# Rows of the last four experts by products with a 0/1 matrix, scatters that do not wait for each other, and a 512-wide second MLP

## The chip, the cores and the metric

The kernel runs on one core of a Trainium2 chip, as one program in one launch. The metric is device time in microseconds (us). The kernel before took 2708.14 us, the median of three runs (2706.81 to 2711.54). The execution that the profiler recorded took 2708.97 us, of which 2707.1 us are the span between the first and the last instruction.

## The reference

512 tokens of width 1024 pass through a hybrid block (state space branch, window attention, and a mixture of experts) and then through a two-layer block with 16 meta tokens ahead of the 512.

```python
def hier_moe(h2, ...):                       # h2: 512 x 1024
    ...                                      # router: two experts of 64 for each token, with a weight each
    def expert_block(args):
        xb, e = args
        hid = jax.nn.silu(xb @ w_gate_e[e]) * (xb @ w_up_e[e])    # 1024 x 256 each
        return hid @ w_down_e[e]                                  # 256 x 1024
    ys = lax.map(expert_block, (xs, block_e)).reshape(n_rows, -1)
    return jnp.zeros_like(h2).at[tok].add(ys * wt[:, None])       # weighted rows back to their tokens
...
def squared_relu_mlp(x, g, w_in, w_out):
    h = rmsnorm(x, g)
    return jnp.square(jax.nn.relu(h @ w_in)) @ w_out              # 1024 -> 4096 -> 1024
...
# second block: h = [meta; x + moe]; h += stick-breaking attention (a_w_qkv, a_w_o); h += mlp 0;
#               h += differential attention; h += mlp 1; the 512 token rows are the output
```

All values are float32. Nothing but the 512 x 1024 result leaves the chip.

## The kernel before

The first block takes the span up to about 700 us, the router and the experts the stretch to about 1300, attention A the stretch to 1660, MLP 0 to 2020, attention B to 2340, and MLP 1 the rest. A framework orders the instructions of each engine once, when the program is built, by its own estimate of durations; `pin` keeps an instruction in program order. Engines then run their lists in that order and wait for each other on semaphores, so an instruction that stands late in its engine's list makes everything wait that needs it.

**Experts.** Each expert has 48 slots. A group of five experts is gathered together: products of a 0/1 matrix `perm` with the tokens (line 787, 16 matmuls in four of five experts) give `xg`, the tokens of the slots, turned. For expert e, `expert_m` (line 928) makes gate and up by 16 float32 matmuls (32 in the trace, where each takes two passes); ACT makes silu (line 935, `lo`), DVE the product (line 936, `sg`); PE turns it (line 943), an engine copies it to `hT`; `expert_d` (line 955) makes the 48 x 1024 result one expert later. ACT and DVE copy its two halves to one of three buffers `ys` (lines 958 and 959), and POOL scatters these rows to the DRAM tile `y_d` with an indirect DMA (line 898). All scatters write the one tile `y_d`, and the framework makes each wait until the one before has landed.

**Weights.** 192 loads of 1 MB on SP's queue (line 910) go into a ring of 14 tiles, in the order in which PE uses them; a load waits for the matmuls that last read its tile.

**Combination.** When all is scattered, SP loads `y_d` back by 8 loads (line 739), DVE multiplies by the token's two weights and adds to `x2` (line 745, 16 instructions 128x512), PE turns the sums (line 750), and `hT` goes to attention A. Its first projections (line 229) need the first `a_w_qkv` weights split into two parts `wh` and `wl` (lines 179 and 180) and the scaled tokens split into `hh` and `hl` (lines 209 and 210).

**MLP 1.** All products with split operands are three matmuls (high by high, low by high, high by low, line 229). In MLP 1 each of them is 256 wide: the first layer takes the 512 tokens in two spans (`HX`), the second takes 256 columns of `w_out` at a time, over eight slices of the 1024 hidden values of a chunk.

## Time and profile before

| what | us |
|---|---|
| median of three runs | 2708.14 |
| profiled execution | 2708.97 |
| its span | 2707.1 |
| first expert to last expert's products | 760 to 1271 |
| last product to attention A at full clock | 1271 to 1320 |
| MLP 1 | 2340 to 2707 |

PE is busy in 94% of the span, with a mean granted clock of 0.977. A granted clock of 1.00 is 2.4 GHz, 0.50 is 1.2 GHz. The trace names its queues and engines as the page does: PE the matrix engine, PEld its weight loads, DVE, ACT and POOL the others, SP the queue of plain DMAs. In a row "idle before" stands in brackets with the instruction that ended it.

### The profile page before, as it was taken

Reading aid. Unit: us, or ns where it says so; the run is one execution under the profiler, and the core shown is the slowest. Engines: PE = TensorE matmul, PEld = TensorE weight load, DVE = VectorE, ACT = ScalarE, POOL = GpSimd, SP = SyncE. Lnnn points to the kernel's source line nnn. Section 1 sums busy time; section 2 is a strip of 40 time slices with the busy share of each in tenths; the row PEclk is TensorE's granted clock in tenths of the full one; section 3 lists DMA queues with packets and bytes.
Section 4 is the critical chain, followed back from the end, with each engine's and each line's share of the span. In section 5 each row is a group of like instructions: output and inputs, shape, how many; then the busy total and the mean of one; then the engine's idle time right before and its main releaser. Section 6 shows DMA issues by size and latency. Waiting matters only on the chain.

```text
span 2707.1 us, 46829 instructions
## 1 busy us (share of the span) xinstructions
PE 2533.1 (94%) x18850; PEld 2180.6 (81%) x18850; DVE 1546.9 (57%) x3266; ACT 1089.3 (40%) x2249; POOL 537.8 (20%) x534
## 2 busy tenths in 40 slices
PE   7998999999889999986789889999999899999999
PEld 5987769879855555543788789999999777899999
DVE  6488676696542222221699887334557878644433
ACT  5356644442311111111477655223335766523321
POOL 0044532130101011111144330001201445100000
PEclk9999999999989999998799999999999999999999
DMA  5233365545399999994411323222231111322221
GB/s 191 90 112 123 108 218 174 174 140 195 110 411 398 419 409 398 415 412 167 177 56 32 102 69 130 87 94 94 94 115 63 32 56 51 115 85 91 93 93 63
DMA packets 111436, 436.92 MB, mean 161 GB/s; under 512 B 16505, under 2 KB 37545, under 8 KB 68976
## 3 DMA queue, kind: packets, MB, share of 16 engines
q1 hardware_dynamic: 105552, 429.20, 43.3%
q0 software_dynamic: 5520, 4.63, 0.7%
q8 instruction: 150, 2.46, 0.4%
q14 instruction: 70, 0.57, 0.1%
q10 hardware_dynamic: 144, 0.07, 0.0%
HBM read 400.52 MB, written 43.79 MB: 164 GB/s over the span
## 4 chain that ended last, share of the span: by engine, by line
PE 52%; DVE 9%; ACT 3%; DMA 3%; issue 2%; POOL 0%; POOLq 0%; DVEq 0%; ACTq 0%; SPq 0%
PE pd L229 35%; PE pd L928 7%; DMA y_d<-ys,idx 3%; PE pm L787 3%; PE pm L955 3%; DVE zd L1927 1%; PE pd L242 1%; DVE wl L180 1%; DVE zt L1915 1%; DVE zd L1916 1%; PE pm L2425 1%; PE pm L943 1%; PE pm L229 1%; PE pm L242 0%; ACT zt L1917 0%
## 5 line engine op out<-in xcount | busy, mean ns | idle before, releaser
L229 PE MATMUL pd<-hh,wh 128*128 128x256 f32 (+2 forms) x1408 | 436.7, 312 | 12.0 <-ACT hh L209 8.5
L229 PE MATMUL pd<-hh,wl 128*128 128x256 f32 (+2 forms) x1408 | 436.9, 311 | 1.0 <-DVE wl L242 1.0
L229 PE MATMUL pd<-hl,wh 128*128 128x256 f32 (+2 forms) x1408 | 436.1, 311 | 0.9 <-DVE hl L210 0.9
L206 ACT ACTIVATE wh<-raw 128x1024 fp32r<-128x1024 f32 (+2 forms) x228 | 222.7, 1022 | 402.6 <-PE pd L229 301.8
L207 DVE TENSOR_TENSOR wl<-raw,wh 128x1024 fp32r<-128x1024 f32 (+2 forms) x228 | 280.3, 1260 | 155.6 <-ACT wh L206 155.4
L229 PEld LDWEIGHTS pd<-hh,wh 128*128 128x128 f32 x1408 | 266.7, 190 | 26.7 <-ACT hh L209 9.2
L229 PEld LDWEIGHTS pd<-hl,wh 128*128 128x128 f32 x1408 | 267.3, 190 | 15.9 <-DVE hl L210 1.6
L229 PEld LDWEIGHTS pd<-hh,wl 128*128 128x128 f32 x1408 | 266.9, 190 | 15.5 <-DVE wl L242 1.9
L229 PE MATMUL pd<-wh,hh 128*128 128x256 f32 (+2 forms) x936 | 266.7, 285 | 4.4 <-DVE vt L2273 1.8
L229 PE MATMUL pd<-wl,hh 128*128 128x256 f32 (+2 forms) x936 | 264.1, 282 | 2.2 <-DVE wl L210 2.2
L229 PE MATMUL pd<-wh,hl 128*128 128x256 f32 (+2 forms) x936 | 264.2, 282 | 0.0
L928 PE MATMUL pd<-mraw,xg 128*48 128x256 f32 x2048 | 237.9, 386 | 0.0
L928 PEld LDWEIGHTS pd<-mraw,xg 128*48 128x48 f32 x2048 | 128.5, 124 | 90.1 <-issue 12.8
L229 PEld LDWEIGHTS pd<-wh,hh 128*128 128x128 f32 (+1 forms) x936 | 170.3, 182 | 10.2 <-issue 2.7
L229 PEld LDWEIGHTS pd<-wl,hh 128*128 128x128 f32 (+1 forms) x936 | 170.2, 182 | 4.5 <-DVE wl L210 2.7
L229 PEld LDWEIGHTS pd<-wh,hl 128*128 128x128 f32 (+1 forms) x936 | 170.0, 182 | 1.9 <-issue 0.2
L898 POOL DMA_INDIRECT y_d<-ys,idx x64 | 60.8, 950 | 474.1 <-DMA y_d<-ys,idx 222.3
L229 PE MATMUL pd<-vh,wl 128*128 128x272 f32 (+1 forms) x512 | 145.1, 284 | 0.0
L229 PE MATMUL pd<-vl,wh 128*128 128x272 f32 (+1 forms) x512 | 144.9, 284 | 0.0
L229 PE MATMUL pd<-vh,wh 128*128 128x272 f32 (+1 forms) x512 | 143.7, 285 | 0.0
L229 PE MATMUL pd<-wl,vh 128*128 128x256 f32 x512 | 143.1, 281 | 0.0
L229 PE MATMUL pd<-wh,vh 128*128 128x256 f32 x512 | 143.0, 281 | 0.0
(573 smaller groups left out, 6269.4 us busy)
## 6 DMA issues: line engine op xcount, KB each, us to landing
mraw<-in_w_moe SPq DMA_DIRECT2D x192, 1024.0 KB
raw<-in_mlp_w_in SPq DMA_DIRECT2D x32, 1024.0 KB
raw<-in_mlp_w_out SPq DMA_DIRECT2D x32, 1024.0 KB
raw<-in_w_xbc SPq DMA_DIRECT2D x12, 1024.0 KB
raw<-in_a_w_qkv SPq DMA_DIRECT2D x12, 1024.0 KB
raw<-in_w_z SPq DMA_DIRECT2D x8, 1024.0 KB
raw<-in_w_gate_in SPq DMA_DIRECT2D x8, 1024.0 KB
bc<-acT_d SPq DMA_DIRECT2D x32, 256.0 KB
```

Source lines behind the costliest of these rows:

```text
L180: self.nc.vector.tensor_tensor(l[:, x], raw[:, x], h[:, x].bitcast(F32), op=ALU.subtract)
L206: nc.scalar.activation(h, src, AF.Copy)
L207: nc.vector.tensor_tensor(l, src, h.bitcast(F32), op=ALU.subtract)
L229: self.nc.tensor.matmul(*a, **kw)
L242: return lambda *a, **kw: pin(f(*a, **kw))
L787: self.pin(nc.tensor.matmul(p[:, 256 * i:256 * i + 256], lhsT=x[2 * t + k // 4][:, (k % 4 + i) * 128:(k % 4 + i + 1) * 128], rhs=perm[:, t ...
L898: self.nc.gpsimd.indirect_dma_start(out=self.y_d[:, :], out_offset=bass.IndirectOffsetOnAxis(ap=rows, axis=0), in_=y[0:64 + self.CAP], in_ ...
L928: self.pin(self.nc.tensor.matmul(p[64 * i:64 * i + self.CAP, 0:256], lhsT=x[:, k], rhs=w[i][:, k], start=k == 0, stop=k == 7))
L943: self.pin(nc.tensor.transpose(pt[:, f * 128:f * 128 + 128], sg[:, f * 128:(f + 1) * 128], self.ident))
L955: self.pin(nc.tensor.matmul(py[64 * m:64 * m + CAP, :], lhsT=hT[:, f * CAP:(f + 1) * CAP], rhs=wd[:, 1024 * f + 512 * m:1024 * f + 512 * m ...
L1915: nc.vector.tensor_scalar(t[:, :n], z[:, :n], 40.0, None, op0=ALU.min)
L1916: nc.vector.tensor_scalar(d[:, :n], z[:, :n], 40.0, 0.0, op0=ALU.subtract, op1=ALU.max)
```

## The change

Six edits:

- The scatters of experts 0 to 59 are declared independent of each other; each waits only for the fourth before it. Experts 60 to 63 are not scattered: four scatters of zero rows, placed at expert 2, fill their places in `y_d`.
- Experts 60 to 63 work in pairs: two experts' `sg` are turned into one tile `hz`, `expert_pair` makes both results (128 slots x 1024), scales them by `last_w` and splits them into `ysp`; `combine` adds them to the turned `x2` in PSUM by products with a 0/1 matrix `last_p` (tokens by slots). `last_rows` builds both from the router's slots, at expert 60.
- `y_d` (4 loads instead of 8) and `x2` are loaded, multiplied and added during the last experts, and the first weights of attention A are loaded among the last expert weights and split at expert 63. The function table load of ACT moves to expert 63 as well.
- From weight number 171 on the ring has the 7 `mr` tiles only.
- A few small instructions of attention A and B are pinned.
- MLP 1 uses 512-wide matmuls: one span in the first layer, 512 columns of `w_out` and four hidden slices at a time in the second; `w_out` is laid out anew outside the kernel.

```diff
-                if e:
+                if 0 < e <= 60:
                     self.expert_d(h, e - 1)
+                if e == 62:
+                    self.expert_pair(hz, 0)
                 if g < NG - 1:
...
+                if e == 63:
+                    self.pin(nc.scalar.preload_act_table_set("natural_log_exp_and_others"))
...
-                h = self.expert_t(sg)
+                if e < 60:
+                    h = self.expert_t(sg)
+                else:
+                    self.expert_t(sg, hz[e // 2 - 30][:, e % 2])
...
+                    for j in range(60, 64):
+                        self.scatter(self.ys[2], self.idx[:, j:j + 1], 1)
...
+                    hz = [self.cb.tile([128, 2, 2, 64], F32, name=f"hz{j}") for j in range(2)]
+                    for j in range(2):
+                        nc.gpsimd.memset(hz[j], 0.0)
+                    self.ysp = [self.cb.tile([128, 2, 1024], F32R, name=f"ysp{j}") for j in range(2)]
...
+                    x2 = [self.cb.tile([128, 2048], F32, name="x2a"), self.st_tile("wl")]
...
+                if e == 60:
...
-            self.expert_d(h, 63)
+                    self.last_rows()
+                if e == 61:
+                    ys = []
+                    for t in range(4):
+                        ys.append(self.st_tile(("raw", "raw", "wh", "raw")[t]))
+                        if t == 0:
+                            self.ahead(self.a_units())
+                        y = nc.sync.dma_start(ys[t].rearrange("p (k c) -> p k c", k=2),
+                                              self.y_d.rearrange("(k t p h) c -> t p k (h c)", k=2, t=4, h=2)[t])
+                        self.after(y, self.scattered)
+                    for t in range(4):
+                        for i in range(2):
...
+                                V.scalar_tensor_tensor(x2[t][:, c], ys[t][:, 1024 * k + 512 * i:1024 * k + 512 * i + 512], self.gw[k][:, t:t + 1], x2[t][:, c],
...
+                if e == 63:
+                    for _ in range(4):
+                        self.tick()
+            self.expert_pair(hz, 1)
...
+    def last_rows(self):
+        nc = self.nc
+        V = self.PV
+        Q, Q1 = [self.mp.tile([128, 4, 256], F32, tag="perm", bufs=2, name="lastq") for _ in range(2)]
+        for t in range(4):
+            for k, x in enumerate((Q, Q1)):
+                V.tensor_scalar(x[:, t], self.lastc, self.slot_of[:, 4 * k + t:4 * k + t + 1], self.gw[k][:, t:t + 1], op0=ALU.is_equal, op1=ALU.mult)
+            V.tensor_tensor(Q[:, t], Q[:, t], Q1[:, t], op=ALU.add)
+        self.last_w = self.mt.tile([128, 2], F32, name="lastw")
+        self.last_p = self.mp.tile([128, 2, 512], F32R, tag="perm", bufs=2, name="lastp")
+        for j in range(2):
+            p = self.P()
+            for t in range(4):
+                self.pin(nc.tensor.transpose(p[:, 128 * t:128 * t + 128], Q[:, t, 128 * j:128 * j + 128], self.ident))
+            V.tensor_reduce(self.last_w[:, j:j + 1], p, axis=AX.X, op=ALU.add)
+            V.tensor_scalar(self.last_p[:, j], p, 0.0, None, op0=ALU.is_gt)
...
+    def expert_pair(self, hz, j):
+        nc = self.nc
+        e = 60 + 2 * j
+        wd = [self.moe_raw(e + x, 2) for x in range(2)]
+        for m in range(2):
+            p = self.P()
+            for f in range(2):
+                for x in range(2):
+                    self.pin(nc.tensor.matmul(p[64 * x:64 * x + 64, :], lhsT=hz[j][:, x, f], rhs=wd[x][:, 1024 * f + 512 * m:1024 * f + 512 * m + 512],
+                                              start=f == 0, stop=f == 1))
+            c = slice(512 * m, 512 * m + 512)
+            self.split_to(self.ysp[j][:, 0, c], self.ysp[j][:, 1, c], p, self.last_w[:, j:j + 1])
...
+        ps = {}
+        def turn(k):
+            ps[k] = self.P()
+            for t in range(4):
+                self.pin(nc.tensor.matmul(ps[k][:, 128 * t:128 * t + 128], lhsT=x2[t][:, k * 128:(k + 1) * 128], rhs=self.ident, start=t == 0, stop=False, skip_group_check=True))
+        turn(0)
+        turn(1)
+        for k in range(8):
+            p = ps.pop(k)
+            for j in range(2):
+                for x in range(2):
+                    self.pin(nc.tensor.matmul(p, lhsT=self.ysp[j][:, x, k * 128:(k + 1) * 128], rhs=self.last_p[:, j], start=False, stop=j == 1 and x == 1, skip_group_check=True))
+            nc.vector.tensor_copy(hT[k][:, 16:528], p)
+            if k < 6:
+                turn(k + 2)
...
+    def scatter(self, y, rows, free=0):
...
+        if free:
+            for o in self.scattered:
+                self.tc.declare_no_dep(x.ins, o.ins, reason="the rows of two blocks are disjoint")
+            if len(self.scattered) > 3:
+                self.after(x, [self.scattered.pop(0)])
+            self.scattered.append(x)
...
+    def next_ring(self):
+        return self.ring[self.mn % len(self.ring)] if self.mn < 171 else ("mr", self.NMP)
...
-    HX = ((16, 272), (272, 528))
+    HX = ((16, 528),)
...
-                W = self.load_split(I["mlp_w_out"][layer, 4 * c + u], 2048)
+                W = self.load_split(I["mlp_w_out"][layer, 4 * c + u], 2048, 4 if last else 8)
...
+                    n, x = divmod(u, 2)
+                    if not x:
+                        out = [self.PD() for _ in range(4)]
                     for t in range(4):
-                        d = acc[t][u // 2][:, (u % 2) * 256:(u % 2) * 256 + 256]
-
...
+                        ts = slice(128 * t, 128 * t + 128)
+                        self.mm3(out[t], lambda k: hid[0][4 * x + k][:, ts], lambda k: hid[1][4 * x + k][:, ts], lambda k: W[0][:, k], lambda k: W[1][:, k],
+                                 K=4, start=not x, stop=x == 1)
+                        if x:
+                            d = acc[t][n]
+                            V.scalar_tensor_tensor(d, out[t], rc[:, t:t + 1], d, op0=ALU.mult, op1=ALU.add)
+                            if c == 3:
+                                nc.sync.dma_start(self.O[128 * t:128 * t + 128, 512 * n:512 * n + 512], d)
```

The lists that the program is built to differ in three places that matter here. First SP's queue from the experts' weights to attention A, before and then after (`w_moe` expert weights, `x_d` the tokens, `y_d` the scattered rows, `a_w_qkv` attention A's weights).

```order
L910 DMA mraw<-in_w_moe 128x2048 x145
L718 DMA meta<-in_meta 16x1024
L910 DMA mraw<-in_w_moe 128x2048 x17
L717 DMA mraw<-x_d 128x1024 x4
L739 DMA mraw<-y_d 128x1024 x8
L140 DMA raw<-in_a_w_qkv 128x2048 x2
```

```order
L1009 DMA mraw<-in_w_moe 128x2048 x140
L745 DMA mraw<-x_d 128x1024 x2
L727 DMA meta<-in_meta 16x1024
L1009 DMA mraw<-in_w_moe 128x2048 x8
L142 DMA raw<-in_a_w_qkv 128x2048
L1009 DMA mraw<-in_w_moe 128x2048 x5
L741 DMA a_norm_g<-in_a_norm_g 128x8
L745 DMA x2a<-x_d 128x1024 x2
L1009 DMA mraw<-in_w_moe 128x2048 x9
L759 DMA mraw<-y_d 128x2x1024 x4
L142 DMA raw<-in_a_w_qkv 128x2048 x2
```

The loads of `x_d`, of the first `a_w_qkv` and of `a_norm_g` moved in among the last 22 expert weights; the loads of `y_d` stand behind the last of them as before.

Then PE's list ahead of attention A: before from expert 61's products on, after from the end of expert 60 on (`sg` products to be turned, `lastq` the tile behind `last_p`, `mraw` weights, and in the row of line 750 the sums).

```order
L928 MATMUL pd<-mraw,xg 48x256 x16
L955 MATMUL pm<-mraw,hT 48x512 x4
L943 MATMUL pm<-consts,sg 128x128 x2
L928 MATMUL pd<-mraw,xg 48x256 x16
L955 MATMUL pm<-mraw,hT 48x512 x4
L943 MATMUL pm<-consts,sg 128x128 x2
L722 MATMUL pm<-consts,meta 128x16 x8
L928 MATMUL pd<-mraw,xg 48x256 x16
L955 MATMUL pm<-mraw,hT 48x512 x4
L943 MATMUL pm<-consts,sg 128x128 x2
L955 MATMUL pm<-mraw,hT 48x512 x4
L750 MATMUL pm<-consts,mraw 128x128 x32
```

```order
L1057 MATMUL pm<-mraw,hT 48x512 x4
L1042 MATMUL pm<-consts,sg 128x128 x2
L749 MATMUL pm<-consts,meta 128x16 x8
L799 MATMUL pm<-consts,lastq 128x128 x8
L1027 MATMUL pd<-mraw,xg 48x256 x16
L1042 MATMUL pm<-consts,sg 128x128 x2
L1027 MATMUL pd<-mraw,xg 48x256 x16
L813 MATMUL pm<-mraw,hz_11792 64x512 x8
L1042 MATMUL pm<-consts,sg 128x128 x2
L1027 MATMUL pd<-mraw,xg 48x256 x16
L1042 MATMUL pm<-consts,sg 128x128 x2
L813 MATMUL pm<-mraw,hz_11793 64x512 x8
```

The 16 matmuls of an expert (`pd<-mraw,xg`) stand in both; the products with `hT` behind each of them have gone from expert 61 on, two groups of eight with `hz` have come, and ahead of expert 61 stand eight transposes of `lastq`. Behind the last row of after come 32 products with the identity (line 826) and 32 with `last_p` (line 833), in turns, and then attention A.

Last DVE's list from the product of expert 60 (before) and from the end of `last_rows` (after) to the first additions (`wl` the low part of attention A's first weights, `ysp` the low part of a pair's result).

```order
L936 TENSOR_TENSOR sg<-lo,pd 48x256
L959 COPY ys<-pm 48x512
L936 TENSOR_TENSOR sg<-lo,pd 48x256
L256 COPY hT<-pm 128x96
L936 TENSOR_TENSOR sg<-lo,pd 48x256
L959 COPY ys<-pm 48x512 x3
L745 SCALAR_TENSOR_TENSOR mraw<-mraw,gw_8083 128x512 x2
L745 SCALAR_TENSOR_TENSOR mraw<-mraw,gw_8084 128x512 x2
```

```order
L126 TENSOR_SCALAR lastp<-pm 128x512
L1061 COPY ys<-pm 48x512 x2
L1035 TENSOR_TENSOR sg<-lo,pd 48x256 x2
L213 SCALAR_TENSOR_TENSOR ysp_11796<-pm,lastw,ysp_11796 128x512
L259 COPY hz_11793<-pm 128x2x48
L213 SCALAR_TENSOR_TENSOR ysp_11796<-pm,lastw,ysp_11796 128x512
L1035 TENSOR_TENSOR sg<-lo,pd 48x256
L183 TENSOR_TENSOR wl<-raw,wh 128x512 x4
L213 SCALAR_TENSOR_TENSOR ysp_11797<-pm,lastw,ysp_11797 128x512
L766 SCALAR_TENSOR_TENSOR x2a<-mraw,gw_8083,x2a 128x512 x2
L766 SCALAR_TENSOR_TENSOR x2a<-mraw,gw_8084,x2a 128x512
L213 SCALAR_TENSOR_TENSOR ysp_11797<-pm,lastw,ysp_11797 128x512
```

Before, the additions to the sums came after the last copies of `ys`. Now the split of a pair's result, the `wl` part and three of the 16 additions stand ahead of the last pair's second split, and 13 additions behind it.

## Rows read from the trace of the kernel before

**Rows 1.** the page, engines' busy time, and the chain that ended last, by line

```profile
PE 2533.1 (94%) x18850; PEld 2180.6 (81%) x18850; DVE 1546.9 (57%) x3266; ACT 1089.3 (40%) x2249; POOL 537.8 (20%) x534
PE pd L229 35%; PE pd L928 7%; DMA y_d<-ys,idx 3%; PE pm L787 3%; PE pm L955 3%; DVE zd L1927 1%; PE pd L242 1%; DVE wl L180 1%; DVE zt L1915 1%; DVE zd L1916 1%; PE pm L2425 1%; PE pm L943 1%; PE pm L229 1%; PE pm L242 0%; ACT zt L1917 0%
```

**Rows 2.** by stretch: us, engines busy, granted clock, DMA share, GB/s

```profile
1160.00:1200.00 40.00, 36.00 (x272) 21.16 (x270) 10.57 (x21) 6.10 (x15) 4.72 (x5) 1.00 1.00 406
1200.00:1245.00 45.00, 29.33 (x183) 15.77 (x180) 6.63 (x13) 6.46 (x13) 5.66 (x6) 0.85 0.77 309
1300.00:1320.00 20.00, 12.13 (x47) 10.76 (x48) 15.04 (x31) 13.98 (x26) 4.55 (x3) 0.50 0.70 255
...
2400.00:2500.00 100.00, 100.00 (x847) 100.00 (x846) 39.65 (x61) 27.80 (x42) 0.00 (x0) 1.00 0.28 96
```

**Rows 3.** PE's timeline: start, duration, work, idle before; experts 10, 20, 56, 57, 60

```profile
837.99 1.29 PE L928 MATMUL pd<-mraw,xg 128*48 128x256 f32 x10
...
910.41 0.86 PE L928 MATMUL pd<-mraw,xg 128*48 128x256 f32 x6
...
1196.20 3.66 PE L928 MATMUL pd<-mraw,xg 128*48 128x256 f32 x32
1203.83 3.66 PE L928 MATMUL pd<-mraw,xg 128*48 128x256 f32 x32
1219.56 0.69 PE L943 MATMUL pm<-consts,sg 128*128 128x128 f32 x2 [8.25 <-DVE sg L936]
1245.25 3.66 PE L928 MATMUL pd<-mraw,xg 128*48 128x256 f32 x32
```

**Rows 4.** what PE waited for, 880 to 1160 us: total, times, longest

```profile
PE pm L787 <- DVE ys L959: 6.1, 7, 0.9
PE pm L943 <- DVE xg L256: 5.3, 7, 0.8
PE pm L943 <- ACT xg L254: 4.6, 7, 0.7
```

**Rows 5.** what ACT waited for, 1160 to 1245 us

```profile
ACT ys L958 <- DMA y_d<-ys,idx: 35.9, 6, 7.8
```

**Rows 6.** the chain of waits, 1160 to 1325 us: start, duration, what

```profile
1163.41 7.74 DMA y_d<-ys,idx
1171.91 6.69 DMA y_d<-ys,idx
...
1277.14 2.59 DMA y_d<-ys,idx
1279.79 3.79 DMA mraw<-y_d
...
1293.45 1.99 DVE mraw L745 x3
```

**Rows 7.** line 910, weight loads issued before 1200 us

```profile
L910 SPq DMA_DIRECT2D mraw<-in_w_moe x180: 327/328/1588, 707.1 to 1199.9; - x180
```

**Rows 8.** groups of instructions by line and shape, 1060 to 1160 us

```profile
L955 PE MATMUL pm<-mraw,hT 128*48 128x512 f32 x112 | 26.4, 592 | 0.0
L936 DVE TENSOR_TENSOR sg<-lo,pd 48x256 f32<-48x256 f32 x14 | 5.9, 422 | 44.6 <-ACT lo L935 44.6
L124 DVE TENSOR_SCALAR perm<-iota,slots 128x256 fp32r<-128x256 f32 x11 | 3.9, 353 | 0.4
```

**Rows 9.** the same, 1245 to 1320 us

```profile
L745 DVE SCALAR_TENSOR_TENSOR mraw<-mraw,gw 128x512 f32<-128x512 f32 x16 | 10.9, 745 | 11.4 <-DMA mraw<-y_d 11.4
L750 PE MATMUL pm<-consts,mraw 128*128 128x128 f32 x32 | 7.3, 403 | 20.1 <-issue 14.9 <-DVE mraw L745 5.1
L210 DVE SCALAR_TENSOR_TENSOR hl<-hT,a_norm_g,hh 128x528 fp32r<-128x528 f32 x8 | 6.7, 873 | 0.1
```

**Rows 10.** PE's timeline of 512-wide matmuls at full clock, 20 from first to last

```profile
36.83 0.39 PE L229 MATMUL pd<-hh,wl 128*128 128x512 f32 x1
...
41.26 0.39 PE L229 MATMUL pd<-hh,wh 128*128 128x512 f32 x1
```

More of the change, by code (lines that the diff above doesn't have):

```diff
@@ L724, in moe @@
                         nc.scalar.activation(hT[k][:, 0:16], pm[:, k * 16:(k + 1) * 16], AF.Copy)
-            self.expert_d(h, 63)
+                    self.last_rows()
[10 more added lines that the diff above has]
+                        for i in range(2):
+                            c = slice(512 * i, 512 * i + 512)
+                            for k in range(2):
+                                V.scalar_tensor_tensor(x2[t][:, c], ys[t][:, 1024 * k + 512 * i:1024 * k + 512 * i + 512], self.gw[k][:, t:t + 1], x2[t][:, c],
+                                                       op0=ALU.mult, op1=ALU.add)
@@ L726, in moe, with st_tile, a_units @@
+                if e == 63:
+                    for _ in range(4):
+                        self.tick()
+            self.expert_pair(hz, 1)
             self.combine(hT, x2)
+            cb.close()
         return hT
+    def st_tile(self, tag):
+        return self.st.tile([128, 2112], F32, tag=tag, bufs=dict(self.ring)[tag], name="mraw")[:, :2048]
+    def a_units(self):
+        W = self.I["a_w_o"]
+        return [(self.I["a_w_qkv"][i + hg], 2048, 8) for hg in range(4) for i in (0, 4, 8)] + [(W[u][:, :1280], 1280, 5) for u in range(4)] \
+            + [(W[u][:, 1280:], 768, 3) for u in range(4)]
@@ L894, in overflow, with after @@
                     self.scatter(y, rc)
-    def scatter(self, y, rows):
-        self.nc.gpsimd.indirect_dma_start(out=self.y_d[:, :], out_offset=bass.IndirectOffsetOnAxis(ap=rows, axis=0), in_=y[0:64 + self.CAP], in_offset=None,
-                                          bounds_check=2047, oob_is_err=False)
+    def after(self, ins, others):
+        for x in others:
+            self.tc.add_manual_dep(ins.ins, x.ins.name, mybir.DependencyInfo(mybir.DependencyClass.Sync, mybir.DependencyReason.DATA), reason="rows")
+    def scatter(self, y, rows, free=0):
+        x = self.nc.gpsimd.indirect_dma_start(out=self.y_d[:, :], out_offset=bass.IndirectOffsetOnAxis(ap=rows, axis=0), in_=y[0:64 + self.CAP], in_offset=None,
+                                              bounds_check=2047, oob_is_err=False)
+        if free:
[4 more added lines that the diff above has]
+            self.scattered.append(x)
     NMP = 7
     ring = [("raw", 3)] * 3 + [("wh", 2), ("wl", 2)] * 2 + [("mr", NMP)] * NMP
+    def next_ring(self):
+        return self.ring[self.mn % len(self.ring)] if self.mn < 171 else ("mr", self.NMP)
     def moe_load(self, n):
@@ L913, in moe_tile @@
     def moe_tile(self):
-        tag, b = self.ring[self.mn % len(self.ring)]
+        tag, b = self.next_ring()
         self.mn += 1
@@ L1675, in layer_a @@
         self.klz = self.kl_tiles([self.la.tile([128, T2], F32R, tag="kl", bufs=2, name="klz") for _ in range(2)])
-        W = self.I["a_w_o"]
-        self.ahead([(self.I["a_w_qkv"][i + hg], 2048, 8) for hg in range(4) for i in (0, 4, 8)] + [(W[u][:, :1280], 1280, 5) for u in range(4)]
-                   + [(W[u][:, 1280:], 768, 3) for u in range(4)])
         self.rest([self.qkv(0, xs, r, sets[0], late)])
```

77 lines of the change are left out of this document (33 added, 44 removed).

## The prediction

> **What bounds the kernel now.** I read the page first: PE is busy 94% of the span, but the chain that ended last holds 3% of it, some 80 us, in scatters [rows 1], so a part of the experts is bound by something else. The table by stretch says where (its columns are PE, PEld, DVE, ACT and POOL): from 1160 to 1200 us PE is busy 36.0 of 40 us at full clock, from 1200 to 1245 only 29.3 of 45 at a clock of 0.85, and from 1300 to 1320 it has 47 instructions at a clock of 0.50, while MLP 1 is PE from end to end [rows 2]. PE's timeline dates the experts. Ten experts from 10 to 20 take 72.42 us, 7.24 each, which is the pace without waits (7.63 with a gather, as 56 to 57, and less in each fifth). From 20 to 57 the 37 experts take 293.42, which is 25.5 above 37 x 7.24. The three from 57 to 60 take 41.42, with one gap of 8.25 us alone [rows 3].
>
> These two losses differ. Between 880 and 1160 us PE's waits are short, 0.8 to 0.9 us, for copies by DVE of an older expert's results [rows 4]: such copies stand behind the newer expert's product in DVE's list. Between 1160 and 1245 ACT waits 35.9 us for scatters to land before it may write `ys` again [rows 5]. The chain there is one scatter after the other, 1163.41 to 1171.15, 1171.91 to 1178.60 and on like that, and at the end again until 1279.79, when the loads of `y_d` start [rows 6].
>
> **Independent scatters.** Without gaps the three experts from 57 to 60 take 7.63 + 7.63 + 7.63 less one gather (2.0; expert 59 has none) = 20.9 us. So 41.42 - 20.9 = 20.5 us go, if ACT finds its buffer free. A scatter lands in 6.7 to 7.7 us with the weights streaming [rows 6]; with three buffers and a pace of 7.24 it has two experts' time, 14.5 us, and the wait for the fourth before it asks less still. The short waits do not go. By the lists, between experts 20 and 59, gathers, transposes and products with `hT` still wait for an older expert's copy: I count 46 gathers and transposes of that kind before and 43 after. I leave the 25.5 us as they are. What is late next is DMA, which works at a share of 1.00 and 406 GB/s up to 1200 us [rows 2]: 180 of the weights were issued by 1199.9 [rows 7], one in 2.6 us, and expert 60 needs numbers 180 and 181 and the three other megabytes queued ahead of them, so it could start at 1199.9 + 5 x 2.6 + 2.6 = 1215.5 at the earliest. Expert 60 starts at 1245.25 - 20.5 = 1224.8 in my sum. I call this T. The ends are 1215.5 and 1245.
>
> **Experts 60 to 63, from T.** Products 3.66 [rows 3], silu, product and turn to T + 6.3. Then `last_rows`, which the trace does not have: eight comparisons at 0.353 and four additions, taken at the 0.422 of a product of the same width [rows 8], 4.5 us of DVE with PE waiting, as the transposes of `lastq` stand ahead of expert 61; with them T + 12.3. Expert 60 to 61 so takes 12.3 in place of 5.8, and what waits behind it on PE is everything. Two more products: T + 20. A pair's 16 passes at 0.236 [rows 8] take 3.8: T + 24; they take the place of four experts' `hT` products and cost nothing more. The ring of seven tiles lets the last weight go when the first pair is done, T + 24; it lands 2.6 later, and the four loads of `y_d`, queued behind it, at about T + 29.5, 32, 34.5 and 37. Expert 63's products end at T + 28, ACT then has silu, table load and `hz`, and the second pair ends at T + 35. On DVE the last split is ready at T + 36, and 13 of the 16 additions stand behind it at 0.745 [rows 9]: 9.7 us, T + 45.5. Only then does the turning of `x2` have all it needs.
>
> **The combination.** 32 products with the identity: the 32 transposes of before took 7.3 us [rows 9] while the clock fell to the 0.50 of 1300 us [rows 2], so 4 to 7.3; I take 6. 32 products 128x512 with `last_p`, at the step of 512-wide matmuls at full clock, (41.26 - 36.83) / 19 = 0.233 [rows 10]: 7.5. PE was nearly idle from T + 35 to T + 45.5; in the kernel before the clock stands at 0.50 after such a stretch [rows 2], so I add 4 (bounds 0 and 13.5, all at half clock). Copies and splits (0.87 each, [rows 9]) run beside it. Attention A starts at T + 45.5 + 17.5 = T + 63, about T + 64 with its first wait: 1289.
>
> Before, attention A had done by 1320 us 47 instructions in 12.13 us at half clock [rows 2], worth 6.1 at full clock: a start at 1313.9. Weights of attention A are now split beforehand, its stuttering start goes with that. The gain so far is 1313.9 - 1289 = 25. Of this 20.5 is the scatters and 4.5 the tail: what pairs and early loads save (no scatters at the end, 1261 to 1279.8, and no splits of weights behind the combination) is mostly paid back by `last_rows`, by the additions behind the second pair and by 64 products for 32 transposes.
>
> **MLP 1.** 847 matmuls 256 wide in 100 us are 0.1181 each [rows 2]. 3072 of them become 1536 at 0.233: 362.7 - 358.2 = 4.5 us. The PE-bound stretch has no other limit: DVE is busy 40 of 100 us. The Trainium skill, "TensorE: Matmul & The Clock Gate", section "Back-to-back issue gap", gives each isolated matmul a fixed 2.5 ns above its columns; by that this edit would be worth 1536 x 2.5 ns = 3.8 us. The rows give 4.5 and I keep them. The other edits, pins and the earlier `a_norm_g`, I put at 0, between -3 and 3: PE waits in neither attention for one of them in a way I could name.
>
> **Sum.** 2708.97 - 25 - 4.5 = 2679.5 by the profiled execution, 0.83 above the median of three; against runs I say 2679.
>
> **Rivals.**
> 1. The short waits go too. With no chain of scatters the copies come earlier than the lists suggest, and only DMA bounds: T = 1215.5, 9 less: 2670. For it: the lists were made for other durations than the chip's. Against: the waits in [rows 4] come from DVE's order alone, and scatters had no part in them.
> 2. The scatters stay one behind the other. They share POOL's queue; if that takes them one at a time at 7 us, ACT keeps about half of its wait, 10 us: 2689. No row has two scatters in flight; their distance of 7.5 us in [rows 6] is set by the wait that goes. The Trainium skill, "DMA: Bandwidth & Descriptors", section "Two DMAs through the same engine are not ordered", says that descriptors of a queue start in order but are pipelined. No row here shows it; it speaks against this rival.
> 3. Slower: the ring of seven tiles starves PE. From expert 57 on a load waits for a tile freed 2.3 experts earlier. If the loads fell back by more than that, each of seven experts would cost three loads in a row and its products, 7.8 + 3.7 = 11.5, instead of 6.9 on average: 7 x 4.6 = 32 us, 2711. It decides from the point where a load lands over 16 us after its tile came free; at 2.6 us a megabyte and four extra megabytes in between that is 13 us at worst, so it should not.
> 4. The change to the experts is worth nothing: the 20.5 us come back in the tail, where the additions or the first splits stall at half clock (13.5 instead of 4, and `y_d` 3.8 us a load [rows 6] instead of 2.6, and 6 more in the start): 2679 + 9.5 + 5 + 6 = 2700.
>
> **Chances and range.** The forecast 0.55, rival 1 0.17, rival 2 0.13, rival 4 0.08, rival 3 0.07. The range takes in rivals 1 and 2 with the bounds of the combination (4 less, 9.5 more) and most of rival 4: 2660 to 2700. The forecast's own is 2672 to 2690. Under 0.2%, 5.4 us, a measurement of this kernel does not tell a change from none: faster 0.88, same 0.05, slower 0.07.
>
> **What would show it.** ACT's wait for `y_d` gone and expert 60 at 1225; about 12 us from expert 60 to 61; 13 additions in a row ahead of the first product with the identity; attention A from its first product at full clock near 1289; MLP 1 with 512-wide matmuls every 0.233 us and PE still 100% busy. It is wrong if expert 60 starts after 1235, if PE waits for weights from expert 57 on, or if MLP 1 gets gaps in which PE waits for a wider tile.

## The result, and the profile after

The kernel after takes 2679.72 us (median of 4 runs, 2677.19 to 2681.70), the kernel before 2709.27 (4 runs, 2706.81 to 2711.54): a ratio of 0.9891, 95% interval 0.9873 to 0.9908. The forecast of 2679 is met in the sum. The stages will show that of its three terms the first is right in the sum though not in its parts, the second (MLP 1) is too small, and the third, the tail behind the experts, has the wrong sign.

The busy times on the page of the kernel after, beside [rows 1]. The chain that ended last can be followed back only to 1294.6 us here, behind the experts, so it says nothing of the scatters; ACT's waits below do.

```profile
PE 2529.9 (95%) x17386; PEld 2111.9 (79%) x17386; DVE 1546.4 (58%) x3218; ACT 1082.4 (40%) x2209; POOL 536.9 (20%) x536
```

Its table by stretch answers to [rows 2]; the columns are the same (stretch, length, PE, PEld, DVE, ACT, POOL with their counts, granted clock, DMA share, GB/s).

```profile
1160.00:1200.00 40.00, 38.38 (x291) 23.28 (x292) 10.28 (x21) 6.40 (x15) 5.64 (x6) 1.00 0.94 368
1200.00:1223.00 23.00, 21.47 (x161) 12.06 (x159) 5.34 (x11) 5.45 (x11) 4.33 (x6) 1.00 0.95 382
1223.00:1252.00 29.00, 23.04 (x145) 11.53 (x144) 11.13 (x24) 4.77 (x18) 3.77 (x4) 0.88 0.89 355
1252.00:1293.00 41.00, 29.38 (x148) 19.88 (x147) 24.72 (x40) 10.09 (x16) 0.00 (x0) 0.83 0.62 233
1293.00:1313.00 20.00, 16.77 (x109) 15.91 (x107) 11.67 (x17) 9.70 (x19) 6.00 (x7) 0.83 0.19 70
2370.00:2470.00 100.00, 100.00 (x434) 81.23 (x433) 39.48 (x45) 27.46 (x34) 0.00 (x0) 1.00 0.29 102
```

Up to expert 60 PE is now busy at full clock (38.4 of 40 us, then 21.5 of 23). The loss has moved: between 1223 and 1293 PE has 52.4 busy us of 70, at a clock of 0.88 and 0.83. MLP 1 still fills PE, with 434 wide matmuls where there were 847.

What ACT waited for, 1160 to 1230 us. Beside [rows 5], the 35.9 us for scatters are gone; ACT now waits for PE, as an engine does that keeps up.

```profile
ACT lo L1034 <- PE pd L1027: 32.2, 9, 5.5
ACT hT L257 <- PE pm L1042: 13.5, 4, 4.7
ACT xg L257 <- PE pm L871: 12.4, 4, 3.4
```

What PE waited for, 883 to 1163 us, answers to [rows 4]: most of the short waits for copies stayed (14.3 us, before 16.0).

```profile
PE pm L1042 <- DVE xg L259: 5.3, 7, 0.8
PE pm L1042 <- ACT xg L257: 4.6, 7, 0.7
PE pm L871 <- DVE ys L1061: 4.4, 5, 0.9
```

PE's timeline from expert 56 to attention A (start, duration, work, in brackets the idle time before it and its releaser), beside [rows 3]. L1027 is an expert's first product, L799 the transposes of `lastq` in `last_rows`, L813 a pair, L826 the products with the identity, L833 those with `last_p`, L232 attention A. The first row is the start of expert 20, and 1200.20 that of expert 57.

```profile
912.77 0.64 PE L1027 MATMUL pd<-mraw,xg 128*48 128x256 f32 x4
...
1192.61 3.66 PE L1027 MATMUL pd<-mraw,xg 128*48 128x256 f32 x32
...
1200.20 3.66 PE L1027 MATMUL pd<-mraw,xg 128*48 128x256 f32 x32
...
1208.68 3.66 PE L1027 MATMUL pd<-mraw,xg 128*48 128x256 f32 x32
...
1223.21 0.63 PE L1027 MATMUL pd<-mraw,xg 128*48 128x256 f32 x2
1225.67 3.44 PE L1027 MATMUL pd<-mraw,xg 128*48 128x256 f32 x29 [1.83 <-DMA mraw<-in_w_moe]
...
1233.12 0.30 PE L799 MATMUL pm<-consts,lastq 128*128 128x128 f32 x1 [1.11 <-DVE lastq L126]
1234.13 0.47 PE L799 MATMUL pm<-consts,lastq 128*128 128x128 f32 x1 [0.71 <-DVE lastq L126]
...
1237.61 5.04 PE L1027 MATMUL pd<-mraw,xg 128*48 128x256 f32 x32
1243.61 0.44 PE L1042 MATMUL pm<-consts,sg 128*128 128x128 f32 x2 [0.96 <-DVE sg L1035]
...
1253.09 3.65 PE L1027 MATMUL pd<-mraw,xg 128*48 128x256 f32 x30 [0.57 <-DMA mraw<-in_w_moe]
...
1260.84 5.34 PE L813 MATMUL pm<-mraw,hz 128*64 128x512 f32 x14 [1.74 <-ACT hz L257]
1268.11 0.46 PE L826 MATMUL pm<-consts,x2a 128*128 128x128 f32 x2 [1.93 <-DVE x2a L766]
1271.32 0.80 PE L826 MATMUL pm<-consts,x2a 128*128 128x128 f32 x2 [2.76 <-DVE x2a L766]
...
1278.77 2.05 PE L833 MATMUL pm<-lastp,ysp 128*128 128x512 f32 x4
...
1292.88 0.28 PE L232 MATMUL pd<-hh,wh 128*128 128x256 f32 x1
...
1300.61 0.39 PE L232 MATMUL pd<-hl,wh 128*128 128x256 f32 x1 [2.69 <-DVE hl L213]
```

Expert 60 starts at 1223.21 instead of 1245.25, 22.0 earlier, and the 8.25 us gap is gone. From expert 20 to 57 it takes 287.4 us, where [rows 3] have 293.4. From there PE meets one small wait after another: weights 1.83, `lastq` 3.1 in four pieces, products of expert 61 in 5.04 instead of 3.66 us behind these, `hz` 1.74, then the additions.

DVE, same kernel, 1259 to 1277 us: the splits of weights (L183), the pair's splits (L213) and the 16 additions (L766). 13 of them stand behind the last split at 1267.87, as the prediction said.

```profile
1259.13 2.50 DVE L183 TENSOR_TENSOR wl<-raw,wh 128x512 fp32r<-128x512 f32 x4 [1.52 <-ACT wh L182]
1265.22 0.75 DVE L213 SCALAR_TENSOR_TENSOR ysp<-pm,lastw,ysp 128x512 fp32r<-128x512 f32 x1 [3.60 <-ACT ysp L212]
1265.89 2.07 DVE L766 SCALAR_TENSOR_TENSOR x2a<-mraw,gw,x2a 128x512 f32<-128x512 f32 x3
1267.87 0.75 DVE L213 SCALAR_TENSOR_TENSOR ysp<-pm,lastw,ysp 128x512 fp32r<-128x512 f32 x1
1268.54 3.39 DVE L766 SCALAR_TENSOR_TENSOR x2a<-mraw,gw,x2a 128x512 f32<-128x512 f32 x5
1271.85 5.38 DVE L766 SCALAR_TENSOR_TENSOR mraw<-mraw,gw 128x512 f32<-128x512 f32 x8
```

All kernels by stage, us, from one profiled execution each. "First `zd`" is DVE's first instruction that writes the tile `zd`, made from attention A's scores; attention A runs from it to the last write of `zd` from scores; "to B's row sums" runs from the last `zd` to attention B's first row sum, B from its first to its last row sum, "MLP 1" from there to the end of the span.

```
                       expert 0   0 to   60 to  63 to        attn  to B's    attn   MLP 1   span
                       starts     60     63     first zd     A     row sums  B
before                 760.3      484.9  17.7   93.4         248.9 491.3     204.4  406.1   2707.1
before, once more      760.1      482.7  19.7   94.7         250.6 491.3     204.6  406.1   2709.7
after                  763.3      459.9  28.7   89.8         248.8 491.1     197.2  397.5   2676.2
after, once more       764.9      460.6  28.7   87.7         248.8 491.0     200.9  397.5   2680.0
MLP 1 alone            761.7      482.3  20.0   93.7         248.9 491.3     204.4  399.7   2702.0
scatters alone         763.9      463.6  17.6   89.7         249.6 491.1     205.4  406.7   2687.7
scatters, once more    760.7      463.3  18.9   94.1         251.2 491.2     200.4  406.7   2686.4
scatters and MLP 1     759.3      463.7  17.6   86.8         249.7 491.1     200.3  400.0   2668.7
```

By the means of the two executions of each kernel: the start of the experts costs 3.9 (the same kernel differs by up to 3.2 there), experts 0 to 60 give 23.6, 60 to 63 cost 10.0, 63 to the first `zd` gives 5.3, attention A and the way to B 1.2, B 5.5, MLP 1 8.6. The sum is 30.3 against 30.3 between the spans.

### The profile page after: what moved, and what is told of

Its sections match the earlier page's. It is cut to its first block, busy times and chain, and to the rows that moved or that the text cites. A ratio compares the mean times of both kernels' runs of the same rounds, so it can differ in the third digit from the quotient of the medians.

```text
span 2676.2 us, 43771 instructions
## 1 busy us (share of the span) xinstructions
PE 2529.9 (95%) x17386; PEld 2111.9 (79%) x17386; DVE 1546.4 (58%) x3218; ACT 1082.4 (40%) x2209; POOL 536.9 (20%) x536
## 4 chain that ended last, share of the span: by engine, by line
PE 38%; DVE 8%; ACT 3%; issue 2%; POOL 1%; DVEq 0%; POOLq 0%; ACTq 0%
PE pd L232 35%; DVE zd L2026 1%; DVE wl L183 1%; PE pd L245 1%; DVE zt L2014 1%; PE pm L2529 1%; PE pm L232 1%; DVE zd L2015 0%; ACT zt L2016 0%; DVE wl L213 0%; ACT zt L2017 0%; DVE dmx L2489 0%; DVE pr L2505 0%; DVE zs L2006 0%; PE pm L245 0%
## 5 line engine op out<-in xcount | busy, mean ns | idle before, releaser
L232 PE MATMUL pd<-hh,wh 128*128 128x512 f32 (+2 forms) x1152 | 393.4, 343 | 4.7 <-DVE zth L1333 3.2
L232 PE MATMUL pd<-hl,wh 128*128 128x512 f32 (+2 forms) x1152 | 393.1, 342 | 2.7 <-DVE hl L213 2.7
L232 PE MATMUL pd<-hh,wl 128*128 128x512 f32 (+2 forms) x1152 | 393.2, 342 | 1.0 <-DVE wl L245 1.0
L232 PE MATMUL pd<-wh,hh 128*128 128x256 f32 (+2 forms) x936 | 265.8, 284 | 2.6 <-DVE tk L259 1.3
L232 PE MATMUL pd<-wh,hl 128*128 128x256 f32 (+2 forms) x936 | 262.8, 281 | 0.0
L232 PE MATMUL pd<-wl,hh 128*128 128x256 f32 (+2 forms) x936 | 262.4, 280 | 0.0
L232 PEld LDWEIGHTS pd<-hh,wh 128*128 128x128 f32 x1152 | 218.5, 190 | 30.0 <-DVE zth L1333 3.4
L232 PEld LDWEIGHTS pd<-hl,wh 128*128 128x128 f32 x1152 | 218.5, 190 | 28.3 <-DVE hl L213 2.9
L1027 PE MATMUL pd<-mraw,xg 128*48 128x256 f32 x2048 | 237.5, 383 | 2.5 <-DMA mraw<-in_w_moe 2.4
L232 PEld LDWEIGHTS pd<-hh,wl 128*128 128x128 f32 x1152 | 218.7, 190 | 26.7 <-DVE wl L245 1.9
L1027 PEld LDWEIGHTS pd<-mraw,xg 128*48 128x48 f32 x2048 | 128.4, 124 | 92.4 <-issue 10.4
L232 PEld LDWEIGHTS pd<-wh,hh 128*128 128x128 f32 (+1 forms) x936 | 169.4, 181 | 8.1 <-issue 2.7
L232 PEld LDWEIGHTS pd<-wl,hh 128*128 128x128 f32 (+1 forms) x936 | 169.4, 181 | 1.7 <-issue 0.2
L232 PEld LDWEIGHTS pd<-wh,hl 128*128 128x128 f32 (+1 forms) x936 | 169.3, 181 | 1.7 <-issue 0.2
L1035 DVE TENSOR_TENSOR sg<-lo,pd 48x256 f32<-48x256 f32 x64 | 27.1, 423 | 222.9 <-ACT lo L1034 222.9
L232 PE MATMUL pd<-vh,wl 128*128 128x272 f32 (+1 forms) x512 | 145.5, 285 | 0.0
L232 PE MATMUL pd<-vl,wh 128*128 128x272 f32 (+1 forms) x512 | 145.3, 285 | 0.0
L232 PE MATMUL pd<-vh,wh 128*128 128x272 f32 (+1 forms) x512 | 143.6, 284 | 0.0
L232 PE MATMUL pd<-wh,xh 128*128 128x256 f32 (+1 forms) x384 | 124.1, 325 | 0.5 <-DVE acc L1399 0.3
```

The costliest lines, as they stand in the source:

```text
L232: self.nc.tensor.matmul(*a, **kw)
L1027: self.pin(self.nc.tensor.matmul(p[64 * i:64 * i + self.CAP, 0:256], lhsT=x[:, k], rhs=w[i][:, k], start=k == 0, stop=k == 7))
L1035: self.nc.vector.tensor_tensor(sg[0:CAP], lo, p[64:64 + CAP, 0:256], op=ALU.mult)
```

## The experiments

**One part at a time.** The second MLP alone (the part of the diff from `HX` on), the free scatters alone (all 64 scatters stay, `declare_no_dep` and the wait for the fourth before; the loads of `y_d` wait for those in flight), and both.

```diff
+        if free:
+            for o in self.scattered:
+                self.tc.declare_no_dep(x.ins, o.ins, reason="the rows of two blocks are disjoint")
+            if len(self.scattered) > 3:
+                self.after(x, [self.scattered.pop(0)])
+            self.scattered.append(x)
...
-        self.scatter(y, self.idx[:, e:e + 1])
+        self.scatter(y, self.idx[:, e:e + 1], 1)
...
-    HX = ((16, 272), (272, 528))
+    HX = ((16, 528),)
```

MLP 1 alone: 

> The kernel before with nothing but the 512-wide second MLP. My prediction priced this edit at 4.5 us, from a step of 0.233 us for a 512-wide matmul in the first block: 2704.8 beside 2709.3. The two traces together say more: from the middle of MLP 1's norm to the end the shift between them grows from 22.3 to 30.9 us, so if the width alone does it, 8.6 us go: 2700.7, with a step near 0.2305. If a part of the 8.6 came from the state in which the stage is entered, this kernel lies between the two.

Measured 2703.63 (2699.83 to 2705.34, 10 runs) against 2710.19, ratio 0.9977 [0.9967, 0.9987]: 6.6 us, and 6.4 in the stage.

Scatters alone: 

> The kernel before with the scatters of all 64 experts declared independent (each waits for the fourth before it) and nothing else; y_d is loaded when the last four have landed. Theory A: the wait chain from expert 57 on is all that the experts' part gains, 18 to 22 us at expert 60, and the last scatters no longer queue up (4 us more); and attention B, whose lists of instructions change with this edit alone, gains the 7.5 us that the after trace has there: 2709.3 - 33 = 2676. Rival B: the pairs and early loads of the whole change are needed for part of the gain at the end, and attention B's gain comes from the pins: 2709.3 - 20 = 2689.

Measured 2682.40 (2676.24 to 2689.55) against 2710.19, ratio 0.9891 [0.9874, 0.9907]: 27.8 us, nearly all that the whole change gives. Its four runs spread over 13 us, so the interval is wide, 25 to 34 us. ACT still has a remainder of its wait, a third of [rows 5], with up to four scatters in flight. PE feels little of it: one wait of 2.3 us for ACT's `lo`, and experts 57 to 60 take 24.4 us, in the kernel after 23.0.

```profile
ACT ys L970 <- DMA y_d<-ys,idx: 10.8, 4, 4.6
```

Both: 

> The kernel before with independent scatters and the 512-wide second MLP, so the whole change without pairs, 0/1 products, early loads, shorter ring and pins. Theory A: the sum of the two parts, 33 + 8.6 = 42 us, 2667, faster than the whole change (2679.7), since its tail was seen to cost 7 us more than before. Rival B: the pairs carry some 10 us: 2689 - 8.6 = 2681, no faster than the whole change.

Measured 2676.04 (2670.59 to 2680.13), ratio 0.9880 [0.9864, 0.9897]. That is as fast as the whole change or a little faster; the ranges overlap. So pairs, `last_rows`, the 0/1 products and the early loads bring nothing on balance. How can that be, when in this kernel PE stands still for the loads of `y_d` behind the last expert? What PE waited for there, 1200 to 1300 us:

```profile
PE pm L751 <- issue: 11.0, 1, 11.0
PE pd L229 <- ACT hh L209: 6.2, 2, 4.3
PE pm L751 <- DVE mraw L746: 5.1, 2, 2.8
```

The eleven idle microseconds are real, but the kernel after loses more than it fills: from expert 60 to the first `zd` this kernel takes 104.4 us (107.3 and 113.0 with the scatters alone), the kernel after 118.5 and 116.4. Some 10 us of that lie between experts 60 and 63 (17.6 against 28.7); the runs "`last_rows` later" and "no pairs" show where they come from.

**The fourth load of `y_d`.** Its tile is one of the staging ring in the kernel after and waits for DVE's splits of weights; here it comes from the ring of weights.

```diff
-                        ys.append(self.st_tile(("raw", "raw", "wh", "raw")[t]))
+                        ys.append(self.st_tile(("raw", "raw", "wh")[t]) if t < 3 else self.moe_tile())
```

> The changed kernel with one edit: the fourth load of y_d goes into a tile of the weight ring instead of the tile that attention A's first weights leave, so that it is issued some 10 us earlier; the lists of all compute engines stay as they are. Theory: the additions on DVE stand behind the second pair's split and run back to back, so the late load costs nothing: 2679.7, within 0.1%. Rival: the late fourth load holds the combination up: up to 5 us less, 2675.

Measured 2678.45 (2676.56 to 2680.75), ratio 0.9882 [0.9865, 0.9898]: as the kernel after. SP's queue after, and in this kernel (start, time from the first to the last issue of the group):

```profile
1248.54 13.47 SPq L759 DMA_DIRECT2D mraw<-y_d  x4
```

```profile
1246.82 2.78 SPq L759 DMA_DIRECT2D mraw<-y_d  x4
```

The load is issued some 11 us earlier and nothing follows from it: DVE's list has the additions behind the pair's splits anyway.

**Additions first.** The same tile, and the 16 additions pinned ahead of the second pair's splits.

```diff
+            for t in range(4):
+                for i in range(2):
+                    c = slice(512 * i, 512 * i + 512)
+                    for k in range(2):
+                        self.PV.scalar_tensor_tensor(x2[t][:, c], ys[t][:, 1024 * k + 512 * i:1024 * k + 512 * i + 512], ...)
+            self.pin_split = True
             self.expert_pair(hz, 1)
+            self.pin_split = False
```

> The changed kernel with the 16 additions pinned on DVE ahead of the second pair's splits, and the fourth load of y_d into the weight ring. Theory: the additions, 11 us in a row, are what the combination waits for from the end of the second pair on (1266 to 1278.8 in after); now they start when the first load lands, near 1258, and the combination starts 5 to 8 us earlier: 2673. Rival: the loads land too late for that (they took 6.6 to 16.3 us to land), the additions wait for them and hold the splits up behind them: no change or slower, 2680.

Measured 2674.96 (2674.40 to 2676.01) against 2709.44, ratio 0.9874 [0.9856, 0.9893]: the shortest but one, 4.8 below the kernel after. DVE's timeline:

```profile
1258.46 5.88 DVE L126 SCALAR_TENSOR_TENSOR x2a<-mraw,gw,x2a 128x512 f32<-128x512 f32 x8
1264.26 5.88 DVE L126 SCALAR_TENSOR_TENSOR mraw<-mraw,gw 128x512 f32<-128x512 f32 x8
1270.17 1.41 DVE L126 SCALAR_TENSOR_TENSOR ysp<-pm,lastw,ysp 128x512 fp32r<-128x512 f32 x2
```

The additions start beside the second pair (1257.76 to 1261.41 us on PE) and run on behind it to 1270.1; only 1.4 us of splits stand behind them. Counted from this kernel's expert 60 (1219.83) they end at 50.3 us, in the kernel after at 54.0. From expert 63 to the first `zd` it is 84.5 us, 5.3 and 3.2 less than in the two profiles of the kernel after.

**`last_rows` later.** Its transposes, reductions and products are moved behind expert 61.

```diff
+        self.lastQ = Q
+
+    def last_rows2(self):
...
                 if e == 61:
+                    self.last_rows2()
```

> The changed kernel with the eight transposes of lastq (and what DVE makes of them) moved behind expert 61's products, so that PE does not stand still for DVE's twelve instructions ahead of expert 61. After has 14.4 us from expert 60 to 61 where the kernel with independent scatters alone has 5.7. Theory: that stall is passed on in full, since everything behind it waits for PE: expert 61 starts about 7 us earlier after expert 60 and the time falls by 5 to 7 us, to 2674. Rival: the end of the experts is bound by the weights' and y_d's loads and by DVE's additions, so the stall was hidden: 2679, no change.

Measured 2678.18 (2676.05 to 2679.67), ratio 0.9887 [0.9868, 0.9905]: 1.5 less than after, and the two ranges overlap. 60 to 63 takes 29.2 us, no less than the 28.7 with the stall, and 63 to the first `zd` 86.9 instead of 89.8 and 87.7. PE's wait for `lastq` is gone; ahead of the products of expert 61 another stands:

```profile
1233.31 5.70 PE L1034 MATMUL pd<-mraw,xg 128*48 128x256 f32 x30 [4.48 <-DMA mraw<-in_w_moe]
```

In the kernel after, the stall for `lastq` hid this one: the load of expert 61's weight that is issued at 1220.8 us takes 16.3 us and lands at 1237.1, and its products start at 1237.61. The weight loads of the kernel after, 1195 to 1262 us (count, size, median us from issue to landing):

```profile
mraw<-in_w_moe SPq DMA_DIRECT2D x15, 1024.0 KB, 16.3
```

So expert 61 is late by its weight, whether PE stalls for `lastq` or not.

**Both.** 

> Both edits of the two runs before in one kernel. Theory: two stalls in a row on one path, so their gains add: 11 to 14 us below the changed kernel, 2667, which would also beat the kernel with independent scatters and the wide MLP alone (2676.0). Rival: with PE earlier, the loads of the last weights and of y_d bound the end: no more than the better of the two, 2673.

Measured 2674.61 (2672.11 to 2677.01), ratio 0.9869 [0.9849, 0.9888]: no more than additions first. PE waits for weights, 1200 to 1300 us:

```profile
PE pd L1035 <- DMA mraw<-in_w_moe: 7.2, 3, 4.5
```

**No pairs.** The kernel after with all 64 experts scattered, the loads of `y_d` behind the last one and the turning by transposes; the weight ring, early splits, pins and MLP 1 stay.

```diff
-            self.expert_pair(hz, 1)
-            self.combine(hT, x2)
+            self.expert_d(h, 63)
+            for t in range(4):
+                y = nc.sync.dma_start(ys[t].rearrange("p (k c) -> p k c", k=2), ...)
+                self.after(y, self.scattered)
+            self.combine(hT, x2, ys)
```

> The changed kernel without the pairs: experts 60 to 63 are scattered like the others (no zero scatters, no last_rows, no 0/1 products), y_d is loaded and added after the last scatter as before; the earlier x2 loads, the shorter ring, attention A's early weights and their split, the pins and the wide MLP stay. Theory: last_rows and the second pair cost 11 us between experts 60 and 63 and give back only 4 behind them, so without them expert 60 to 63 takes 17.7 instead of 28.7 us, and the early weights still save the stuttering start of attention A: 2679.7 - 12 = 2668, the fastest of all. Rival: without the pairs PE stands idle through scatter and load of y_d, and what the early weights save goes with it: 2676, as with independent scatters and wide MLP alone, or slower.

Measured 2676.41 (2670.56 to 2677.50) against 2710.44, ratio 0.9868 [0.9846, 0.9890]. Here too the idle time is in the open (12.46 us), and the total is that of the kernel after or less. PE's timeline:

```profile
1251.03 3.44 PE L1005 MATMUL pd<-mraw,xg 128*48 128x256 f32 x29 [1.58 <-DMA mraw<-in_w_moe]
...
1271.65 0.44 PE L812 MATMUL pm<-consts,x2a 128*128 128x128 f32 x1 [12.46 <-DVE x2a L807]
...
1284.07 0.79 PE L232 MATMUL pd<-hh,wh 128*128 128x256 f32 x2
```

The expectation was that experts 60 to 63 would fall back to 17.7 us without the pairs. They take 27.7. So `last_rows` and the pairs together account for 1 of the 10 us there. PE waits for weights instead, 1200 to 1300 us:

```profile
PE pd L1005 <- DMA mraw<-in_w_moe: 8.6, 4, 4.1
```

What the weight loads on SP's queue waited for, 1195 to 1250 us, in this kernel, in the kernel after, and in that with scatters and MLP 1 alone, whose experts run at the same pace:

```profile
SPq L987 <- PE pd L1005: 20.9, 4, 9.2
```

```profile
SPq L1009 <- PE pd L1027: 26.4, 6, 9.4
```

```profile
SPq L922 <- PE pd L940: 0.3, 1, 0.3
```

With the ring of seven tiles the last loads wait for PE to free a tile, with the ring of 14 hardly at all. The kernels with the short ring and the loads that were moved ahead (3 MB of `x_d` and `a_w_qkv`) take 27.7 to 29.3 us from expert 60 to 63, in eight profiles; those without take 17.6 to 20.0, in six. Which of the two edits it is, ring or earlier loads, no run separates, and the wait for tiles speaks for the ring.

**The old second MLP in the kernel after.**

```diff
-    HX = ((16, 528),)
+    HX = ((16, 272), (272, 528))
```

> The changed kernel with the 256-wide second MLP of before. Theory: the width alone is worth 8.6 us wherever it stands (trace of after against before), so 2679.7 + 8.6 = 2688. Rival: the 6.6 us that the width alone gave in the kernel before, 2686, or my prediction's 4.5, 2684.

Measured 2683.00 (2681.46 to 2684.88), ratio 0.9900 [0.9880, 0.9919]: 3.3 above the kernel after, and 5.5 in the stage (403.0 against 397.5).

**The same kernels once more.** Attention B is 7 us shorter in the first profile of the kernel after, which no step had foreseen. Is it the lists, or chance?

Before: 

> The kernel before, unchanged, profiled once more. In dispute: attention B took 204.4 us in the profile of the kernel before, 205.4 with the free scatters alone, 197.2 in the kernel after (first to last row sum). Theory A, spread between executions: here attention B takes anything from 197 to 205 us, the span follows it, and the kernels differ in it by chance. Theory B, the instruction lists of the new kernel make it shorter: 203.5 to 205.5 us here, as before.

After: 

> The kernel after, unchanged, profiled once more. Theory A: attention B anywhere from 197 to 205 us. Theory B: 196 to 198.5 us, as in the first profile of it. The experts' stretch is the same for both: expert 60 within 2 us of 1223.2, 60 to 63 within 0.5 of 28.7 us.

Scatters alone: 

> Before with free scatters alone, profiled once more. Theory A: attention B anywhere from 197 to 205 us. Theory B: within 1 us of its first 205.4. The median of its timed runs, 2682.4, stands 5.3 us below the span of its first profile, which speaks for A: 200 to 203 expected.

Spans 2709.7, 2680.0 and 2686.4; attention B 204.6, 200.9 and 200.4 us. Scatters alone differs from itself by 5.0 us and the kernel after by 3.7, so chance has that size. But the kernel before stood at 204.4 and 204.6, and all profiles of the kernel after and its variants between 197.2 and 201.6: a part of 3 us or more may be the lists. What it is stays open.

## Why the prediction came out right, step by step

**Independent scatters: mechanism right, size right only in the sum.** A gain of 20.5 was said for expert 60's start, and it is 22.0 by the first profiles, 19.7 by the means of two. ACT's wait went, PE was busy up to 1223 us, and scatters alone gives 27.8 us of time. The parts are not as said. Experts 57 to 60 take 23.0 and 22.7 us, said 20.9. The 25.5 us between experts 20 and 57 that were to stay shrink by 6.0: 293.4 in both profiles before, 287.4 and 287.5 after, 289.1 in all three with the free scatters but not the rest. And expert 0 starts 2.9 us later. That these nearly cancel is luck. Rival 1 (the short waits go too) so came true in part, 6 of its 9 us: PE's short waits between 905 and 1205 us are 15.1 us after and 20.0 before. Rival 2 (the queue takes the scatters one at a time) would have left expert 60 some 10 us later and falls. POOL issues scatters while others are in flight:

```profile
1186.34 0.94 POOL L987 DMA_INDIRECT y_d<-ys,idx  x1 [11.81 <-DVE ys L1061]
1187.59 0.94 POOL L987 DMA_INDIRECT y_d<-ys,idx  x1 [0.30 <-issue]
```

These land at 1193.0 and 1194.8, and a third is issued at 1190.70. By the Trainium skill, "DMA: Bandwidth & Descriptors", section "Two DMAs through the same engine are not ordered", descriptors within one queue of one DMA engine start in order but are pipelined; the trace agrees in so far as three scatters are in flight at once, each for 6.6 to 7.2 us.

**From expert 60 on: wrong sign.** Said was a tail that gives 4.5 us. From expert 60 to the first `zd` it costs 4.7 by the means of two (7.4 by the first profiles). With T = 1223.2:

- 60 to 61: 14.4 us, said 12.3. DVE's work for `last_rows` is 4.5 us, as said, and the 2.1 are mostly the 1.83 us wait for the rest of expert 60's weight. But the step took the weights to be there, and expert 61's lands only at T + 13.8: with `last_rows` out of the way its products still start at T + 13.9, with a wait of 4.48 us.
- Pair 1 ends at T + 28.4, said T + 24. The other 2.3 are expert 61's products, 5.04 instead of 3.66 behind PE's idle time (1.4), and 0.96 for `sg`. The granted clock was 0.50 (1.2 GHz) from 1235 to 1239 us, behind 4 us (1231 to 1235) in which PE was busy for 1.8, and 1.00 again from 1241; the step had no term for that.
- Pair 2 ends at T + 43.0, said T + 35. A further 3.6. Of these 1.2 come up to the end of expert 63's products, the wait of 0.57 for weights among them. The other 2.4 come behind it, 9.4 us where 7 were said: the step had 3.2 for silu, table load and `hz`, and here PE waits 0.92 for `sg` and 1.74 for `hz`, which ACT copies only behind the table load and four splits, and the pair meets a granted clock of 0.68 (14 passes in 5.34 us; by the 0.236 of the step 3.3).
- The last addition ends at T + 54.0, said T + 45.5: the same 8 us, carried on, and 1.4 more for the last split, which is done 2.4 us behind the pair (said 1). The 13 additions stand where they were said to; they take 8.8 us, said 9.7.
- Attention A's first product is at T + 69.7, said T + 63. The combination behind the additions takes 15.6 us, said 17.5. It starts at full clock (1.00 from 1293 to 1298 us), but then meets a stall of 2.69 for `hl`, since ACT takes six squares (3.32 us) ahead of the last two `hh`, and behind the stall the granted clock is 0.52 from 1303 to 1309.

So two steps of the tail failed, though the total came out. "With them T + 12.3" and "two more products: T + 20" took every weight to be there and charged the delay to `last_rows`. Without `last_rows` ahead of it expert 63 still starts 29.2 us behind expert 60, and without pairs or `last_rows` 27.7: 9 of the 10 us between experts 60 and 63 stay without the pairs, and the waits of PE and of the loads put them on the shorter ring and the loads moved ahead. And "T + 24, T + 35, T + 45.5" took its intervals from PE's work and one queue, while most handovers at this end have a wait of 0.6 to 2.8 us, and the clock is lower behind them (0.88 and 0.83 by stretch). Rival 4, the gain that comes back in the tail, was given 0.08 and 2700. Its direction was right and its size half: the tail came out 9 to 12 us above the forecast, where it had 20.

**MLP 1: mechanism right, term too small.** Said 4.5 us; alone 6.4 in the stage and 6.6 by the medians, in the kernel after 8.6 in the stage. The rows of 2370 to 2470 us give the step: 434 matmuls in the kernel after, 431 in that with scatters and MLP 1.

```profile
2370.00:2470.00 100.00, 100.00 (x431) 80.61 (x431) 39.29 (x44) 27.46 (x34) 0.00 (x0) 1.00 0.26 92
```

That is 0.2304 and 0.2320 us, and not the 0.233 of [rows 10], which was taken from another stage. Against twice the 0.1181 of before, 1536 of them give 8.9 and 6.5 us, which is what the stages show. So the term was mis-sized by a step read elsewhere. Why matmuls step a little faster in the kernel after is open; its variant with the old second MLP has that too (403.0 against 406.1), so it is not the width. The Trainium skill, "TensorE: Matmul & The Clock Gate", section "Back-to-back issue gap", has a fixed 2.5 ns for an isolated matmul, by which 1536 fewer give an estimated 3.8 us; the stages show more, 5.5 to 6.7 for the width.

**Rival 3, a starved PE, came in part.** Its 32 us did not come, but PE's waits for weights from expert 59 on are 0.87, 1.83 and 0.57 us, which the prediction had named as a sign that it is wrong, and the stall for `lastq` hides more: without it 4.5 and 4.1 us ahead of expert 61. The step that ruled this rival out had 13 us at worst until a load lands. Here 16.3 us pass from the issue alone.

The sum was right by luck, because errors cancelled. By the means of two, the tail was forecast too good by 9.2 us, the start of the experts by 3.9 and experts 57 to 60 by 2.9; against these stand 6.0 from experts 20 to 57, 4.1 from MLP 1 and 6.7 from attention A and B, a good part of which is chance.

## What to carry to other kernels

A false dependence between writes to one memory tile costs its whole chain once the work between two writes is no longer than a transfer (here 7.24 us an expert, 6.7 to 7.7 us a scatter): declare disjoint writes independent before restructuring anything, since here this one edit gave 27.8 of 29.6 us. Idle time of an engine that waits for a result (11 to 12 us here) is worth only what is left of it when the work that is to fill it has its own handovers: count every handover from engine to engine, each with its wait and the clock behind it, and not the work alone. Room and bandwidth that such work takes from a prefetch have a price too: with half the ring and 3 MB moved ahead, the last weights came late and cost about as much as the idle time was worth. When a stall is removed and nothing gets faster, look for the wait that it hid. In a list order set ahead, look for long independent work (13 additions) that stands behind a late producer, and put it in front: that was 4.8 us for no work at all (3.2 to 5.3 in the stage).

## What the runs showed of the hardware that was not expected

- Three indirect scatters in flight at once (four are allowed) land in 6.6 to 7.2 us each, no slower than one at a time (6.7 to 7.7). With the free scatters and little else ACT still waits 10.3 to 10.8 us for them over 1160 to 1230, in the kernel after not at all, before 35.9 over 1160 to 1245.
- The same kernel on the same inputs differs by 3.7 to 5.0 us in attention B alone (197.2 and 200.9; 205.4 and 200.4), while MLP 1 repeats to 0.1 us (397.5 twice, 406.1 twice).
- A 512-wide matmul at full clock steps by 0.2304 to 0.2320 us in a long run of them; two 256-wide ones take 0.2361.
- After about 3 us of stalls in four pieces between 1232 and 1237 us the granted clock was 0.50 until 1239 and 1.00 from 1241 on, and the 32 products of expert 61 took 5.04 us, where 3.66 is their time at full clock.
- With a ring of seven 1 MB tiles the weight loads waited 21 to 26 us for a free tile between 1195 and 1250 us; with 14 tiles and the same pace of experts 0.3 us.
